# First phase of a hybrid decoder layer from a transposed x, the norm's factor applied to results, and other PSUM banks around the merge

## The chip, the cores and the metric

The kernel runs on one core of a Trainium2 chip. The metric is the device time of one execution in microseconds (us), lower is better. The core's engines are TensorE (PE in the profile; its weight loads are PEld), VectorE (DVE), ScalarE (ACT), GpSimd (POOL) and SyncE (SP), which here only issues DMA transfers.

## The reference

One layer on 512 tokens of width 1024, all in float32. A shared RMS-normalised input h goes through one wide projection, whose columns feed two branches: an mLSTM (queries and keys through a convolution, values v_ml, output gates o_ml, input and forget gates if_pre) and a sliding-window attention with 16 query and 4 key/value heads. The branches are merged with sigmoid gates, projected, and followed by an MLP and a gated embedding.

```python
def reference(x, p, norm_mix_g, w_in, conv_qk, b_if, mlstm_norm_g, sinks, w_branch_a, w_branch_b,
              w_out, norm_mlp_g, w_up, w_down, norm_ple_g, w_ple_gate, w_ple_proj, final_norm_g):
    h = rmsnorm(x, norm_mix_g[i])
    proj = h @ w_in[i]
    qk_ml, v_ml, o_ml, if_pre, q_sw, k_sw, v_sw, g_a, g_b = jnp.split(proj, split_idx, axis=-1)
    ...
    gates = (if_pre + b_if[i].astype(if_pre.dtype)).astype(jnp.float32)
    ...
    h_ml = mlstm_chunkwise(q_ml, k_ml, v_ml.reshape(B, S, ML_HEADS, ML_DV), ig, lf)
    ...
    y_a = jax.nn.sigmoid(o_ml) * h_ml
    y_b = swa_with_sinks(...)
    merged = jax.nn.sigmoid(g_a) * (y_a @ w_branch_a[i]) + jax.nn.sigmoid(g_b) * (y_b @ w_branch_b[i])
    x = x + merged @ w_out[i]
    u = rmsnorm(x, norm_mlp_g[i]) @ w_up[i]
    x = x + jnp.square(jax.nn.relu(u)) @ w_down[i]
    gate = jax.nn.sigmoid(rmsnorm(x, norm_ple_g[i]) @ w_ple_gate[i])
    x = x + gate * (p[i].astype(x.dtype) @ w_ple_proj[i])
    return rmsnorm(x, final_norm_g)
```

The norm multiplies each token's row by a factor r (one over the root of its mean square) and each column by norm_mix_g. Since r is one number for a token, h @ W equals r times ((x * norm_mix_g) @ W).

## The kernel before

**Products.** Every float32 operand is split into a high part (a cast to a shorter format, on ScalarE, L138) and a low part (the rest, a subtraction on VectorE, L139), by split (L135). Each product is three matmuls: high by high, high by low, low by high (pairs, L159; chain, L167, is the line of nearly every matmul). Weights come in pieces of 128x1024, 512 KB: load_w (L151) issues one DMA from SyncE into a buffer wr (four of them), casts into wh and subtracts into wl (four each). A piece is used by 24 matmuls of 512 columns.

**Start.** x arrives by token: four tiles xt of 128 tokens by 1024, with three pieces of w_vsif (the columns of the attention's values and of the eight gate inputs, 264 wide) queued between the first and the second. stir (L244) runs idle matmuls from the first instant. For each token tile, norm (L270) squares and sums on ScalarE and gives r; scaled (L281) multiplies by r and norm_mix_g on VectorE; turn (L286) transposes 128x128 blocks on TensorE; high (L294) and low (L298) split the result into hT, the normalised input with the 1024 columns on the partitions. products (L318) then makes the 128x264 block of values and gate inputs of that token tile, 24 matmuls into one PSUM bank, and values (L322) copies it out (vs, gt). A block manual_schedule (L330) fixes the order of TensorE, ScalarE and VectorE up to here; SyncE follows the text.

**Keys and output gates.** Two key products (L384) follow, split at once. Gate inputs are transposed (L420), and VectorE and ScalarE run scans over time on them (L424 to L447); their results are transposed again as gg and em (L502). o_proj (L411) makes eight output-gate products o0 to o7: 24 matmuls, a sigmoid on ScalarE into a tile sgo, a DMA from GpSimd to a DRAM tile god. o_bank (L404) gives o0, o1, o6, o7 a bank of the pool g and o2 to o5 the four banks of two two-bank tiles psa: o2 and o3 share one, o4 and o5 the other.

**vml.** The mLSTM values use a scheme of seven products instead of eight for a 2x2 block product (seven, L519). Its inputs are parts of hT (A11, A12, A22) and four sums S1 to S4 of such parts (h_sum, L470; their float32 source hf, L462, adds high and low part again; the split sums are hS).

**Merge.** For eight blocks, 24 matmuls of w_a, then VectorE multiplies by a gate (L920), GpSimd adds the other branch's term (L921), and the sum is split into mg. Then the PSUM pools close and a new pool pq opens with three two-bank pairs (pair, L936) and two single banks g. The w_out products (L951) go to two pairs for the first half of the columns, and to one pair and two g banks for the second (L958).

Outside the manual blocks a scheduler orders each engine's instructions by the text and by issue_after; each engine then runs its instructions strictly in that order, each waiting for what it needs.

Of the kernel before, what the change touches and what calls it, by code (L numbers as in the profile page):

```python
# [36 lines left out]
def block_kernel(  # L37
    ctx: ExitStack,
    tc: tile.TileContext,
    x: bass.AP,  # L40
    p: bass.AP,
# [183 lines left out]
    xt = [tk("xt")[:, :D] for _ in range(NT)]  # L225

    def load_x(m, n=1):
        for c in range(n):
            o = slice(c * D // n, (c + 1) * D // n)
            nc.sync.dma_start(out=xt[m][:, o], in_=x[m * P : (m + 1) * P, o])  # L230
# [13 lines left out]
    def stir(n):  # L244
        for i in range(n):
            tc.keep_in_program_order(T.matmul(idle[:, :P], ones, ones, start=True, stop=True))

    stir(9)
    gmix = [ps_a()[:, :512] for _ in range(2)]
    for c in range(2):  # L250
        T.matmul(gmix[c], ones, grow[:, c * 512 : (c + 1) * 512], start=True, stop=True)
    stir(2)
# [10 lines left out]
    vs = []  # L263
    gt = c1.tile([P, NT, 8], F32, name="gt")
    h2, hT = big_hl("h")
    hf = []
    xns = [tok_scratch("xn") for _ in range(NT)]
    rss = {}

    def norm(m):  # L270
        ss = small("ss", 1)
        A.activation(xns[m], xt[m], AF.Square, accum_out=ss)
        sd = small("sd", 1)
        A.activation(sd, ss, AF.Sqrt, bias=eps_t, scale=1.0 / D)
        rss[m] = small("rs", 1, 5)
        V.reciprocal(rss[m], sd)

    def scaled(m):
        for c in range(2):
            o = slice(c * 512, (c + 1) * 512)  # L280
            V.scalar_tensor_tensor(xns[m][:, o], xt[m][:, o], rss[m], gmix[c], ALU.mult, ALU.mult)  # L281

    def turn(m, kq):
        ps = ps_t()
        for k in range(4):
            T.transpose(ps[:, k * P : (k + 1) * P], xns[m][:, kq * 512 + k * P : kq * 512 + (k + 1) * P], ident)  # L286
        return ps

    def parts(m, kq):
        o = slice(4 * kq, 4 * kq + 4)  # L290
        return [t[:, o, m * P : (m + 1) * P] for t in h2]

    def high(m, kq, ps):
        return A.copy(parts(m, kq)[0], ps.rearrange("p (k c) -> p k c", k=4)).ins  # L294

    def low(m, kq, ps):
        hi, lo = parts(m, kq)
        return V.tensor_sub(lo, ps.rearrange("p (k c) -> p k c", k=4), r32(hi)).ins  # L298

    wvh = [wp.tile([P, 1024], F32R, tag="wh", bufs=WB, name=nm("wh"))[:, : n * 264] for _, n in vsif]  # L300
    wvl = [wp.tile([P, 1024], F32R, tag="wl", bufs=WB, name=nm("wl"))[:, : n * 264] for _, n in vsif]

    def w_high(i):
        A.copy(wvh[i], wv[i][:, : vsif[i][1] * 264])

    def w_low(i):
        V.tensor_sub(wvl[i], wv[i][:, : vsif[i][1] * 264], r32(wvh[i]))

    def products(m, order):
        ps = ps_g()  # L310
        where = {k0 + k: (i, k) for i, (k0, n) in enumerate(vsif) for k in range(n)}
        done = 0
        for kind, ks in order:
            for k in ks:
                i, c = where[k]
                act = hT[k][1 if kind == "lo h" else 0][:, m * P : (m + 1) * P]
                w = (wvl if kind == "lo w" else wvh)[i][:, c * 264 : (c + 1) * 264]
                last_mm[0] = T.matmul(ps[:, :264], act, w, start=done == 0, stop=done == 3 * KT - 1)  # L318
                done += 1
        return ps  # L320

    def values(m, ps):  # L322
        t = sp.tile([P, 256], F32, tag="vs", bufs=4, name=nm("vs"))
        A.copy(t, ps[:, :256])
        vs.append(t)
        return V.tensor_add(gt[:, m, :], ps[:, 256:264], bif)

    early, late, every = range(4), range(4, 8), range(8)
    plain = [("hi", early), ("lo w", early), ("lo h", early), ("hi", late), ("lo w", late), ("lo h", late)]
    with tc.manual_schedule(engines={mybir.EngineType.PE, mybir.EngineType.Activation, mybir.EngineType.DVE}):  # L330
        norm(0)
        w_high(0)
        scaled(0)
        w_low(0)
        t_ = [turn(0, kq) for kq in range(2)]
        high(0, 0, t_[0])
        low(0, 0, t_[0])
        w_high(1)
        high(0, 1, t_[1])
        w_low(1)  # L340
        low(0, 1, t_[1])
        w_high(2)
        w_low(2)
        norm(1)
        scaled(1)
        ps0 = products(0, [("hi", early), ("lo w", range(3)), ("lo h", early), ("hi", late), ("lo w", range(3, 8)), ("lo h", late)])
        t_ = [turn(1, kq) for kq in range(2)]
        norm(2)
        high(1, 0, t_[0])
        high(1, 1, t_[1])  # L350
        low(1, 0, t_[0])
        low(1, 1, t_[1])
        scaled(2)
        ps1 = products(1, plain)
        norm(3)
        values(0, ps0)
        scaled(3)
        t_ = [turn(2, kq) for kq in range(2)]
        q = [ps_a()[:, :512] for _ in range(2)]
        for kq in range(2):  # L360
            high(2, kq, t_[kq])
            low(2, kq, t_[kq])
        for kq in range(2):
            for k in range(4):
                T.transpose(q[kq][:, k * P : (k + 1) * P], xns[3][:, kq * 512 + k * P : kq * 512 + (k + 1) * P], ident)
        for kq in range(2):
            turned = [high(3, kq, q[kq]), low(3, kq, q[kq])]
        values(1, ps1)
        ps2 = products(2, plain)
        ps3 = products(3, plain)  # L370
# [8 lines left out]

    HALF = [slice(0, 64), slice(64, 128)]
    with tc.issue_after(turned[0]), tc.issue_after(turned[1]), tc.issue_after(turned[2]):
        keys = []  # L384
# [929 lines left out]
```

## Time and profile before

| | us |
|---|---|
| median of 3 runs (894.09 to 894.49) | 894.4 |
| the profiled execution | 894.35 |
| its span on the core | 892.5 |
| TensorE busy | 881.7 |
| VectorE busy | 646.3 |
| ScalarE busy | 450.2 |
| GpSimd busy | 24.3 |

The granted TensorE clock of the profiled run was 0.999 of full on average. The span is the time between the first and the last instruction that the profiler saw; the execution lasts 1.85 us longer. Busy times of different engines overlap. DMA moved 100.5 MB, 113 GB/s over the span, and was denser at the start: 284, 192 and 171 GB/s in the first three fortieths.

### The profile page before, as it was taken

The numbers are of one execution on the slowest core, as the hardware profiler recorded it, in microseconds if no ns is written. First come the engines' busy times: TensorE is split into PE (matmuls) and PEld (weight loads), VectorE is DVE, ScalarE is ACT, GpSimd is POOL, SyncE is SP. The second block draws the span as 40 slices with busy tenths as digits, with TensorE's granted clock in tenths as the row PEclk, the third lists the DMA queues.
The fourth block names the chain that finished last, engine by engine and source line by source line (L and its number), as shares of the span: only waits on it lengthen the run. The fifth ranks groups of instructions, "written<-read, shape, count | busy, mean of one in ns | idle before, by whom it ended". The sixth has DMA issues, their size and how long they took to land.

```text
span 892.5 us, 12113 instructions
## 1 busy us (share of the span) xinstructions
PE 881.7 (99%) x4672; PEld 740.2 (83%) x4672; DVE 646.3 (72%) x1029; ACT 450.2 (50%) x757; POOL 24.3 (3%) x42
## 2 busy tenths in 40 slices
PE   9999999999999999999999999999999999999996
PEld 8888899998878777788878888888888888888886
DVE  6875687864887887668634679757966885798466
ACT  6463444443667577764323545434434533444843
POOL 1011000000000000001300000000000000000000
PEclk9999999999999999999999999999999999999999
DMA  8552234335121232325353611630352054102402
GB/s 284 192 171 89 69 115 148 142 127 171 59 69 50 71 106 84 118 95 188 118 189 95 230 54 37 201 117 24 97 186 95 1 178 153 47 25 79 135 1 95
DMA packets 29965, 100.50 MB, mean 113 GB/s; under 512 B 4173, under 2 KB 4685, under 8 KB 29906
## 3 DMA queue, kind: packets, MB, share of 16 engines
q1 hardware_dynamic: 27938, 93.15, 31.3%
q0 software_dynamic: 1824, 6.30, 2.0%
q8 instruction: 37, 0.61, 0.3%
q10 hardware_dynamic: 144, 0.26, 0.1%
q14 instruction: 22, 0.18, 0.1%
HBM read 91.30 MB, written 8.40 MB: 112 GB/s over the span
## 4 chain that ended last, share of the span: by engine, by line
PE 77%; DVE 1%; ACT 0%; issue 0%; DVEq 0%
PE psg L167 37%; PE psp L167 23%; PE psg L768 8%; PE pst L167 2%; PE pst L743 1%; PE psa L696 1%; PE psa L730 1%; PE psa L167 1%; PE pst L842 1%; PE psp L947 1%; PE pst L894 0%; DVE gb L882 0%; DVE vh L139 0%; PE psp L989 0%; ACT wh L138 0%
## 5 line engine op out<-in xcount | busy, mean ns | idle before, releaser
L138 ACT CAST wh<-wr 128x1024 fp32r<-128x1024 f32 x134 | 140.6, 1052 | 209.0 <-PE psg L167 61.6
L139 DVE TENSOR_TENSOR wl<-wr,wh 128x1024 fp32r<-128x1024 f32 x134 | 168.5, 1262 | 100.8 <-ACT wh L138 93.8
L167 PE MATMUL psg<-x,wh 128*128 128x512 f32 x512 | 158.4, 390 | 0.0
L167 PE MATMUL psp<-wh,uf 128*128 128x512 f32 x448 | 139.1, 390 | 0.0
L167 PEld LDWEIGHTS psg<-x,wh 128*128 128x128 f32 x512 | 96.1, 188 | 19.8
L167 PE MATMUL psg<-x,wl 128*128 128x512 f32 x256 | 99.7, 389 | 0.0
L167 PEld LDWEIGHTS psp<-wh,uf 128*128 128x128 f32 x448 | 84.1, 188 | 17.4
L167 PE MATMUL psp<-wl,uf 128*128 128x512 f32 x224 | 87.2, 389 | 0.0
L138 ACT CAST wh<-wd 128x1024 fp32r<-128x1024 f32 x44 | 46.3, 1054 | 58.0 <-PE psp L167 26.3
L768 PE MATMUL psg<-h,wh 128*128 128x512 f32 x192 | 62.3, 399 | 0.0
L139 DVE TENSOR_TENSOR wl<-wd,wh 128x1024 fp32r<-128x1024 f32 x44 | 53.5, 1219 | 4.7 <-ACT wh L138 4.5
L167 PEld LDWEIGHTS psg<-x,wl 128*128 128x128 f32 x256 | 48.1, 188 | 9.9
L167 PE MATMUL psa<-h,wh 128*128 128x256 f32 (+1 forms) x256 | 55.2, 312 | 0.5 <-ACT p L617 0.4
L167 PEld LDWEIGHTS psp<-wl,uf 128*128 128x128 f32 x224 | 42.1, 188 | 8.6
L139 DVE TENSOR_TENSOR uf<-F,uf 128x1792 fp32r<-128x1792 f32 (+2 forms) x20 | 33.0, 1650 | 21.8 <-ACT uf L138 21.8
L167 PEld LDWEIGHTS psa<-h,wh 128*128 128x128 f32 x256 | 41.9, 191 | 4.0 <-ACT p L617 1.2
L167 PE MATMUL psg<-yb,wh 128*128 128x512 f32 x128 | 43.1, 408 | 0.3 <-DVE gb L882 0.2
L768 PEld LDWEIGHTS psg<-h,wh 128*128 128x128 f32 x192 | 35.4, 188 | 8.1 <-issue 0.4
L138 ACT CAST uf<-F 128x1792 fp32r<-128x1792 f32 (+2 forms) x20 | 27.9, 1397 | 26.4 <-DVE F L1023 26.2
L1009 DVE SCALAR_TENSOR_TENSOR rt<-psg,rB 128x512 f32<-128x512 f32 x32 | 22.0, 688 | 25.6 <-PE psg L167 25.6
L167 PE MATMUL psg<-ya,wh 128*128 128x512 f32 x128 | 40.5, 395 | 0.0
L167 PE MATMUL psg<-h,wh 128*128 128x512 f32 x128 | 39.9, 393 | 0.0
(289 smaller groups left out, 1729.7 us busy)
## 6 DMA issues: line engine op xcount, KB each, us to landing
wr<-in_w_up SPq DMA_DIRECT2D x32, 512.0 KB, 3.4
wd<-in_w_down SPq DMA_DIRECT2D x24, 512.0 KB, 4.3
wr<-in_w_o SPq DMA_DIRECT2D x8, 512.0 KB, 4.2
gd<-gr POOLq DMA_DIRECT2D x8, 512.0 KB, 2.9
wr<-in_w_qsw SPq DMA_DIRECT2D x8, 512.0 KB, 4.3
wr<-in_w_qkml SPq DMA_DIRECT2D x8, 512.0 KB, 3.4
wr<-in_w_b SPq DMA_DIRECT2D x8, 512.0 KB, 3.4
gl<-gd SPq DMA_DIRECT2D x8, 512.0 KB, 3.4
```

What stands on the lines that cost most here:

```text
L138: done = A.copy(dst[0], src)
L139: V.tensor_sub(dst[1], src, r32(dst[0]))
L167: last_mm[0] = T.matmul(ps, l, r, start=first and i == 0, stop=last and i == len(ops) - 1, skip_group_check=parts)
L696: T.matmul(o, q[x][HALF[ab], n * P : (n + 1) * P], keys[kp][y][HALF[ab], k0 : k0 + 256], start=i == 0, stop=i == 2)
L730: T.transpose(pt[:, c : c + P], lm3[:, g, j * P : (j + 1) * P], ident)
L743: T.matmul(o[HALF[ab], m * 256 : (m + 1) * 256], vs[n + m + 1 - nk + j][:, c : c + 64], pTs[m][:, j * 512 + ab * 256 : j * 512 + (ab + 1) ...
L768: T.matmul(ps, l, r, start=k == 0 and j == 0, stop=k == KT - 1 and j == 2)
L842: T.matmul(psc[:, n0:], qk[4 + h][:, n0 : n0 + P], qk[h][:, n0:], start=True, stop=True)
L947: T.transpose(ps[:, m * P : (m + 1) * P], xk[m][:, k * P : (k + 1) * P], ident)
L1009: V.scalar_tensor_tensor(a, ps, 0.0, rB, ALU.max, ALU.mult)
```

## The change

x is now passed twice, by token and transposed (x_t, four pieces of 256 columns by 512 tokens). Values, gate inputs, keys and the first three output gates are computed from xg, the split of x_t * norm_mix_g, which has no r in it. Tokens arrive later and only give the sums of squares. From these r4 (128x4, r of each token) is made; four matmuls of ones by a diagonal of r4 (psr) give rows, the factors of all 512 tokens on every partition. Values and gate inputs are multiplied by r4, keys (kt) and the first three output gates by rows. h_rows makes the normalised x in place and splits it into hT, which o3 to o7 and all that follows use. The values are made k by k into four banks. The manual block now runs to o4, and includes SyncE. S1 to S4 come from the normalised x itself. In the merge the add is on VectorE, and the new pool's two g banks are taken before the pairs.

```diff
+    gmix = cp.tile([P, KT], F32, name="gmix")
+    nc.scalar.dma_start(out=gmix, in_=g_mix)
...
-    load_x(0, 2)
-    nc.sync.dma_start(out=grow[:1, :], in_=g_mix)
-    vsif = [(0, 3), (3, 3), (6, 2)]
-    wv = [load_raw(w_vsif[0, :, k0 * 264 : (k0 + n) * 264], n * 264) for k0, n in vsif]
-    load_x(1)
-    load_x(2)
-    load_x(3)
+    xT = [tk("xT")[:, :D].rearrange("p (two c) -> p two c", two=2) for _ in range(4)]
+    vsif = [(0, 2), (2, 3), (5, 3)]
...
+    def o_close(i, ps, by=None):
+        t = act_f("sgo")
+        if by is not None:
+            last_v[0] = V.tensor_mul(t, ps, by).ins
+            ps = t
+
+        def gate():
+            A.activation(t, ps, AF.Sigmoid)
+            nc.gpsimd.dma_start(out=god[i // 2][:, i % 2, :], in_=t)
+
+        return gate
...
+    def x_split(k):
+        split(xg[k], x_part(k), gmix[:, k : k + 1])
...
+    def squares(m, t):
+        A.activation(t, t, AF.Square, accum_out=ss4[:, m : m + 1])
...
+    with tc.manual_schedule(engines={ENG.PE, ENG.Activation, ENG.DVE, ENG.SP}):
+        for i in range(10):
+            T.matmul(idle[:, :P], ones, ones, start=True, stop=True)
+        nc.sync.dma_start(out=xT[0][:, 0, :], in_=x_t[0, :, :S])
+        for i, (k0, n) in enumerate(vsif):
+            wv.append(load_raw(w_vsif[0, :, k0 * 264 : (k0 + n) * 264], n * 264))
+            if i == 0:
+                nc.sync.dma_start(out=xT[0][:, 1, :], in_=x_t[0, :, S:])
+            else:
+                nc.sync.dma_start(out=xT[i].rearrange("p a b -> p (a b)"), in_=x_t[i])
+        nc.sync.dma_start(out=xT[3].rearrange("p a b -> p (a b)"), in_=x_t[3])
+        kraw = [load_raw(w_ksw[0], KT * P)]
+        xm = [tok_scratch("xm") for _ in range(NT)]
+        for m in range(NT):
+            if m == 2:
+                kraw.append(load_raw(w_ksw[1], KT * P))
+            nc.sync.dma_start(out=xm[m], in_=x[m * P : (m + 1) * P, :])
...
+        sd4, r4 = small("sd", NT), small("r4", NT)
+        A.activation(sd4, ss4, AF.Sqrt, bias=eps_t, scale=1.0 / D)
+        V.reciprocal(r4, sd4)
+
+        vps = [t[:, :264] for t in four_a()]
+        for k in range(KT):
+            i, c = where[k]
+            w = [t[i][:, c * 264 : (c + 1) * 264] for t in (wvh, wvl)]
+            for j, (l, rt) in enumerate(pairs(xg[k], w)):
+                for m in range(NT):
+                    T.matmul(vps[m], l[:, m * P : (m + 1) * P], rt, start=k == 0 and j == 0, stop=k == KT - 1 and j == 2)
+        kps = [ps_t(), ps_t()]
+        for _ in products_of(kps[0], kw[0], xg):
+            pass
+        late = products_of(kps[1], kw[1], xg)
+        for _ in range(12):
+            next(late)
+        dg = act_f("dg")
+        psr = ps_g()
+        for m in range(NT):
+            o = slice(m * P, (m + 1) * P)
+            V.tensor_scalar_mul(dg[:, o], ident, r4[:, m : m + 1])
+            T.matmul(psr[:, o], ones, dg[:, o], start=True, stop=True)
+        for _ in late:
+            pass
+        ow = [load_w(w_o[0], KT * P, KT)]
+        rows = act_f("rows")
+        A.copy(rows, psr)
+        for m in range(NT):
+            t = sp.tile([P, 256], F32, tag="vs", bufs=4, name=nm("vs"))
+            A.activation(t, vps[m][:, :256], AF.Copy, scale=r4[:, m : m + 1])
+            vs.append(t)
+            V.scalar_tensor_tensor(gt[:, m, :], vps[m][:, 256:264], r4[:, m : m + 1], bif, ALU.mult, ALU.add)
+        h2, hT = big_hl("h")
+
+        def h_rows(i):
+            for j in range(2):
+                V.scalar_tensor_tensor(xT[i][:, j, :], xT[i][:, j, :], gmix[:, 2 * i + j : 2 * i + j + 1], rows, ALU.mult, ALU.mult)
+            split([t[:, 2 * i : 2 * i + 2, :] for t in h2], xT[i])
+
+        h_rows(0)
+        ow.append(load_w(w_o[1], KT * P, KT))
+        h_rows(1)
+        h_rows(2)
+        ow.append(load_w(w_o[2], KT * P, KT))
+        h_rows(3)
+        ow.append(load_w(w_o[3], KT * P, KT))
         for i in range(2):
-            ps = proj_T(w_ksw, i, ps_t)
+            t = act_f("kt")
+            V.tensor_mul(t, kps[i], rows)
             keys.append(act_hl("kk"))
-            split(keys[i], ps)
+            split(keys[i], t)
+        ops = [o_open(i, xg, ow[i]) for i in range(3)]
+        gates = [o_close(i, ops[i], rows) for i in range(3)]
+        rows_last = last_v[0]
+        ow.append(load_w(w_o[4], KT * P, KT))
+        for i in (3, 4):
+            gates.append(o_close(i, o_open(i, hT, ow[i])))
+            if i == 3:
+                o_last = last_mm[0].ins
+    for gate in gates:
+        gate()
...
+    with tc.issue_after(o_last):
+        pgi, pgf = ps_t(), ps_t()
...
-        G.tensor_tensor(sg, sg, t2[i], ALU.add)
+        V.tensor_add(sg, sg, t2[i])
...
+    first_g = [ps_g(), ps_g()]
...
-            pv = [a[:, 0, :], a[:, 1, :], ps_g(), ps_g()]
+            pv = [a[:, 0, :], a[:, 1, :], *first_g]
```

TensorE's first instructions, in the kernel before: idle matmuls (ones), transposes of a token tile (xn by ident), and the first products (h by the vsif weights wh and wl, into one bank).

```order
L246 MATMUL psg_122<-ones 128x128 x2
L286 MATMUL pst_163<-ident,xn_141 128x128 x4
L286 MATMUL pst_168<-ident,xn_141 128x128 x4
L318 MATMUL psg_189<-wh_145,h_139 128x264 x3
L318 MATMUL psg_189<-wh_146,h_139 128x264
L318 MATMUL psg_189<-wl_148,h_139 128x264 x3
```

The same place after; xg_116 and xg_117 are high and low part of the first 128 columns of x, psa_213 and psa_214 the four banks of the four token tiles.

```order
L306 MATMUL psg_108<-ones 128x128 x10
L348 MATMUL psa_213<-wh_171,xg_116 128x264 x2
L348 MATMUL psa_214<-wh_171,xg_116 128x264 x2
L348 MATMUL psa_213<-wl_172,xg_116 128x264 x2
L348 MATMUL psa_214<-wl_172,xg_116 128x264 x2
L348 MATMUL psa_213<-wh_171,xg_117 128x264 x2
L348 MATMUL psa_214<-wh_171,xg_117 128x264 x2
```

The transposes are gone, and the products go through all four token tiles before the next 128 columns.

VectorE behind the values, in the kernel before: the float32 sums hf, the subtractions of the two keys kk, the sums s, and the low parts wl of output-gate weights.

```order
L466 TENSOR_TENSOR hf_563<-h_139,h_140 128x1024
L139 TENSOR_TENSOR kk_392<-pst_360,kk_391 128x512
L474 TENSOR_TENSOR s_95_565<-hf_557 128x4x128
...
L139 TENSOR_TENSOR wl_614<-wr_611,wh_613 128x1024
L139 TENSOR_TENSOR wl_647<-wr_644,wh_646 128x1024
L139 TENSOR_TENSOR kk_427<-pst_395,kk_426 128x512
L424 COPY ig_456<-pst_446 4x512
```

The same place after; wl_414 and wl_424 are the low weights of o2 and o3, xT_106 the last block of h_rows, sgo_515 to sgo_519 the multiplied products of o0 to o2.

```order
L140 TENSOR_TENSOR wl_414<-wr_411,wh_413 128x1024
L375 SCALAR_TENSOR_TENSOR xT_106<-xT_106,gmix,rows_377 128x512 x2
L140 TENSOR_TENSOR h_392<-xT_106,h_391 128x1024
L140 TENSOR_TENSOR wl_424<-wr_421,wh_423 128x1024
L387 TENSOR_TENSOR kt_427<-pst_311,rows_377 128x512
L140 TENSOR_TENSOR kk_430<-kt_427,kk_429 128x512
L387 TENSOR_TENSOR kt_433<-pst_312,rows_377 128x512
L140 TENSOR_TENSOR kk_436<-kt_433,kk_435 128x512
L262 TENSOR_TENSOR sgo_515<-psg_439,rows_377 128x512
L262 TENSOR_TENSOR sgo_517<-psg_464,rows_377 128x512
L262 TENSOR_TENSOR sgo_519<-psa_489,rows_377 128x512
L140 TENSOR_TENSOR wl_524<-wr_521,wh_523 128x1024
```

Normalising x, both keys and three multiplications now stand in one row, with the weights of o1 to o3 between them and those of o4 behind.

ScalarE as vml begins, in the kernel before: sigmoids of o4 to o7 (sgo), casts of vml weights (wh), and the two copies p of the first product A11.

```order
L414 ACTIVATE sgo_707<-psa_610 128x512
L138 CAST wh_900<-wr_848 128x1024
L414 ACTIVATE sgo_761<-psa_610 128x512
L414 ACTIVATE sgo_795<-psg_764 128x512
L138 CAST wh_916<-wr_850 128x1024
L414 ACTIVATE sgo_829<-psg_798 128x512
L138 CAST wh_935<-wr_840 128x1024
L572 COPY p_164_892<-psa_856 128x512
L572 COPY p_165_894<-psa_856 128x512
```

The same place after; hS are the high parts of the sums, sgo_744, sgo_778 and sgo_812 the sigmoids of o5, o6 and o7.

```order
L139 CAST wh_918<-wr_823 128x1024
L139 CAST hS_677<-s_115_672 128x512
L139 CAST hS_681<-s_115_672 128x512
L139 CAST wh_936<-wr_825 128x1024
L139 CAST hS_685<-s_114_667 128x512
L139 CAST hS_689<-s_114_667 128x512
L266 ACT_TABLE_LOAD
L266 ACTIVATE sgo_744<-psa_490 128x512
L266 ACTIVATE sgo_778<-psg_753 128x512
L266 ACTIVATE sgo_812<-psg_787 128x512
L560 COPY p_159_875<-psa_839 128x512
L560 COPY p_160_877<-psa_839 128x512
```

The sigmoids of o5 to o7 stood among the weight casts and stand now behind four of the hS casts, one weight cast more (wh_936) and a table load.

## Rows read from the trace of the kernel before

**Rows 1.** The page's first part: busy time, share, instructions of each engine.

```profile
PE 881.7 (99%) x4672; PEld 740.2 (83%) x4672; DVE 646.3 (72%) x1029; ACT 450.2 (50%) x757; POOL 24.3 (3%) x42
```

**Rows 2.** Waits of TensorE, whole kernel: what waited for what: total, times, longest.

```profile
PE psp L167 <- ACT wh L138: 0.9, 1, 0.9
```

**Rows 3.** Timeline of TensorE, start: start, duration, instruction, count, idle before.

```profile
0.99 4.21 PE L246 MATMUL psg<-ones 128*128 128x128 f32 x18 [0.99 <-POOL ones L199]
...
8.82 1.14 PE L318 MATMUL psg<-wh,h 128*128 128x264 f32 x4
...
19.03 0.73 PE L318 MATMUL psg<-wh,h 128*128 128x264 f32 x4
...
24.92 0.62 PE L167 MATMUL pst<-h,wh 128*128 128x512 f32 x2
```

**Rows 4.** Timeline of TensorE in vml: A11, the first S2 matmuls, A12.

```profile
81.61 0.39 PE L167 MATMUL psa<-wh,h 128*128 128x512 f32 x1
...
87.05 0.39 PE L167 MATMUL psg<-wh,hS 128*128 128x512 f32 x1
...
88.41 0.47 PE L167 MATMUL psa<-wh,h 128*128 128x512 f32 x1
```

**Rows 5.** Timeline of TensorE, merge: the last w_a matmul, the first of w_out.

```profile
447.60 0.39 PE L167 MATMUL psg<-ya,wl 128*128 128x512 f32 x1
448.86 0.47 PE L167 MATMUL psp<-wh,mg 128*128 128x512 f32 x1 [0.88 <-ACT wh L138]
```

**Rows 6.** Timeline of SyncE's issues, start: three vsif pieces, then x.

```profile
2.08 1.29 SPq L148 DMA_DIRECT2D wr<-in_w_vsif  x3
3.41 1.71 SPq L230 DMA_DIRECT2D xt<-in_x  x3
```

**Rows 7.** DMA issues of 3.2 to 3.8 us: size, us from issue to landing.

```profile
xt<-in_x SPq DMA_DIRECT2D x1, 512.0 KB, 6.9
wr<-in_w_vsif SPq DMA_DIRECT2D x1, 264.0 KB, 6.0
```

**Rows 8.** Stretch table: length, busy PE, PEld, DVE, ACT, POOL, clock, DMA, GB/s.

```profile
8.80:24.80 16.00, 15.42 (x119) 14.33 (x120) 12.92 (x25) 11.88 (x23) 0.00 (x0) 1.00 0.81 286
```

**Rows 9.** Timeline of TensorE: ones by diagonal in a later norm, and what follows.

```profile
501.03 0.61 PE L989 MATMUL psp<-dg,ones 128*128 128x128 f32 x4
501.40 0.47 PE L167 MATMUL psg<-x,wl 128*128 128x512 f32 x1
```

**Rows 10.** Groups by shape, 0 to 130 us, ScalarE: busy, mean ns, idle before.

```profile
L138 ACT CAST wh<-wr 128x1024 fp32r<-128x1024 f32 x27 | 28.4, 1055 | 45.1 <-PE psa L167 15.5 <-PE psg L167 10.9 <-PE pst L167 7.1
...
L414 ACT ACTIVATE sgo<-psg 128x512 f32<-128x512 f32 x4 | 2.3, 593 | 0.0
...
L324 ACT COPY vs<-psg 128x256 f32<-128x256 f32 x4 | 1.5, 376 | 1.0 <-PE psg L318 1.0
...
L414 ACT ACT_TABLE_LOAD x1 | 1.3, 1283 | 0.0
```

**Rows 11.** The same view, VectorE.

```profile
L139 DVE TENSOR_TENSOR wl<-wr,wh 128x1024 fp32r<-128x1024 f32 x26 | 31.5, 1222 | 22.9 <-ACT wh L138 16.1 <-issue 6.5
...
L326 DVE TENSOR_TENSOR gt<-psg,bif 128x8 f32<-128x8 f32 x4 | 0.6, 157 | 0.1
```

**Rows 12.** Line 680, VectorE, operands in SBUF: shortest, median, longest ns.

```profile
L680 DVE SCALAR_TENSOR_TENSOR acc<-acc,sg x8: 682/684/685, 332.0 to 337.5; 128x512 f32<-128x512 f32 x8
```

**Rows 13.** Timeline of ScalarE: three hS casts in a row.

```profile
54.34 1.67 ACT L138 CAST hS<-s 128x512 fp32r<-128x512 f32 x3
```

**Rows 14.** Timeline of VectorE, merge: the last multiplication by the gate.

```profile
448.02 0.69 DVE L920 TENSOR_TENSOR sga<-psg,gl 128x512 f32<-128x512 f32 x1 [1.64 <-PE psg L167]
```

**Rows 15.** Timeline of TensorE: the last matmul of the kernel.

```profile
885.04 0.28 PE L167 MATMUL psg<-wh,x 128*128 128x256 f32 x1
```

**Rows 16.** Stretch table behind it (columns as rows 8; the clock stands third-last).

```profile
889.00:889.50 0.50, 0.00 (x0) 0.00 (x0) 0.00 (x0) 0.00 (x0) 0.00 (x0) 1.00 0.29 106
889.50:890.00 0.50, 0.00 (x0) 0.00 (x0) 0.00 (x0) 0.00 (x0) 0.00 (x0) 0.82 1.00 381
```

More of the change, by code (lines that the diff above doesn't have):

```diff
@@ L40, in block_kernel @@
     x: bass.AP,
+    x_t: bass.AP,
     p: bass.AP,
@@ L222, in cols @@
         return t
[L225 to L230, printed above, removed]
-    load_x(0, 2)
-    nc.sync.dma_start(out=grow[:1, :], in_=g_mix)
-    vsif = [(0, 3), (3, 3), (6, 2)]
-    wv = [load_raw(w_vsif[0, :, k0 * 264 : (k0 + n) * 264], n * 264) for k0, n in vsif]
-    load_x(1)
-    load_x(2)
-    load_x(3)
+    xT = [tk("xT")[:, :D].rearrange("p (two c) -> p two c", two=2) for _ in range(4)]
+    vsif = [(0, 2), (2, 3), (5, 3)]
+    where = {k0 + k: (i, k) for i, (k0, n) in enumerate(vsif) for k in range(n)}
     bif = c1.tile([P, 8], F32, name="bif")
-    nc.sync.dma_start(out=bif, in_=b_if.broadcast_to([P, 8]))
     idle = ps_g()
[L244 to L252, printed above, removed]
     def rstd_of(ss, n):
@@ L261, in rstd_of @@
         return rs
[L263 to L372, printed above, removed]
@@ L409, in o_bank, with o_open @@
         return obanks[i - 2]
-    def o_proj(i):
-        ps = proj_T(w_o, i, lambda: o_bank(i))
-        t = act_f("sgo")
-        A.activation(t, ps, AF.Sigmoid)
-        nc.gpsimd.dma_start(out=god[i // 2][:, i % 2, :], in_=t)
-    pgi, pgf = ps_t(), ps_t()
-    for m in range(NT):
-        T.transpose(pgi[:4, m * P : (m + 1) * P], gt[:, m, :4], ident)
-        T.transpose(pgf[:4, m * P : (m + 1) * P], gt[:, m, 4:], ident)
+    last_v = [None]
+    def o_open(i, acts, w):
+        ps = o_bank(i)
+        mm_T(ps, w, acts)
+        return ps
@@ new lines, in block_kernel, with x_part, w_split @@
+    xg = [act_hl("xg") for _ in range(KT)]
+    wv, wvh, wvl = [], [], []
+    ss4 = small("ss", NT)
+    def x_part(k):
+        return xT[k // 2][:, k % 2, :]
+    def x_split(k):
+        split(xg[k], x_part(k), gmix[:, k : k + 1])
+    def w_split(i):
+        n = vsif[i][1] * 264
+        wvh.append(wp.tile([P, 1024], F32R, tag="wh", bufs=WB, name=nm("wh"))[:, :n])
+        wvl.append(wp.tile([P, 1024], F32R, tag="wl", bufs=WB, name=nm("wl"))[:, :n])
+        split([wvh[i], wvl[i]], wv[i][:, :n])
@@ new lines, in block_kernel, with proj_T @@
+    for gate in gates:
+        gate()
+    gml = cols(g_ml, KT, "gml", c1)
+    gmlp = cols(g_mlp, KT, "gmlp")
+    gple = cols(g_ple, KT, "gple")
+    cw = cols(conv, KT * 4, "cw", c1)
+    sink = c1.tile([P, 16], F32, name="sink")
+    nc.sync.dma_start(out=sink, in_=sinks.broadcast_to([P, 16]))
+    def proj_T(wd, i, bank=ps_g):
+        ps = bank()
+        mm_T(ps, load_w(wd[i], KT * P, KT), hT)
+        return ps
+    with tc.issue_after(o_last):
+        pgi, pgf = ps_t(), ps_t()
+        for m in range(NT):
+            T.transpose(pgi[:4, m * P : (m + 1) * P], gt[:, m, :4], ident)
+            T.transpose(pgf[:4, m * P : (m + 1) * P], gt[:, m, 4:], ident)
```

96 lines of the change are left out of this document (50 added, 46 removed).

## The prediction

> **What bounds the kernel now.** I read the page first: TensorE is busy 881.7 of 892.5 us, VectorE 72%, ScalarE 50% [rows 1]. Then TensorE's waits: the longest late one is 0.9 us [rows 2]. So the end time is TensorE's own line of matmuls; a change counts only where it makes that line start earlier, grow, or stop. Then I read, stage by stage, what TensorE does where the change cuts in: the start [rows 3], vml [rows 4], the merge [rows 5]. The profiled execution took 894.35 us, 1.85 more than its span; I sum against 894.35, which is the median of 894.4 to within 0.05.
>
> **1. Keys start earlier.** Before, TensorE does its first product at 8.82 and, token block by token block, reaches the first key matmul at 24.92 [rows 3]. After, k by k, no normalised tile is needed. k=0 and 1 need the first 776 KB and are done early; k=2 needs the tile xT1, with which 256+264+256+396+512 = 1684 KB have been sent. In the queue before, 1572 KB had landed with the third vsif load (issued near 2.95 as the last of three from 2.08, 6.0 us to land: 8.95) and 2084 KB with the x tile behind it (3.41+6.9 = 10.3) [rows 6, 7]. Between them by bytes: 9.25. One 512-column cast, 0.59 to 0.62, gives 9.9. Then 72 matmuls (six k, four token blocks, three terms) at 0.123, which is (24.92-19.03)/48 [rows 3]: keys from 18.75, **-6.2**. The other tiles keep pace at the 286 GB/s of that stretch [rows 8] (xT2 near 12.5, used from 12.85). A landing 1.3 us off either way moves this term by as much.
>
> **2. The norm's factor.** Four matmuls of ones with a diagonal (psr) are added between 36 and 12 key matmuls. Four records of that kind took 501.40-501.03 = 0.37 [rows 9]; eight and the change of weights, **+0.9**. They need the tokens: 3.1 MB more after 12.9 at 286 GB/s is 23.9; square 1.05 (the pass of a 128x1024 cast [rows 10]) and small steps 0.8 give 25.8. TensorE gets there at 18.75+36x0.2267 = 26.9, at the pace of 24 matmuls in 87.05-81.61 [rows 4]. In time by 1.1 us. So psr ends at 27.8 and the keys at 30.5.
>
> **3. What is behind psr on VectorE.** Now h, keys and gates come late and in one row. psr read at 28.0, rows copied by 28.6 (0.59); four vs copies (0.376) and gt steps (0.157) in turn, about 1.8 [rows 10, 11]: 30.4. A block of h_rows is two SBUF steps (0.684 each, near enough 1.3 a pair [rows 12]), a cast 1.05, a subtraction 1.22 [rows 10, 11] and hand-overs: 3.6. Four blocks and three weight subtractions (1.15 when queued back to back) end at 48.25. Two keys, each multiply 0.69 [rows 14], cast 0.58, subtract 0.68: 52.3. Three sgo multiplies: 54.2.
> TensorE has 48 matmuls for o0 and o1 (10.9): at o2 by 41.4. o2's weights come between blocks 2 and 3: cast 42.2, subtraction 43.5. Idle 0.8 and 0.9, **+1.7**. o2 ends at 48.55. o3 writes the other half of o2's tile, psa_489's neighbour, and its first matmul waits for sgo_519, the last row of the VectorE piece shown with the diff: 54.25. **+5.7**. Both ends: nothing if that chain were 7.4 shorter, 8.6 in all if each block took 0.3 more. I take 7.4, since every pass in it has its own row. Behind the waiting matmul stand o3 to o7, everything. The transposes of gates, gg and em, now stand inside o7, and the gate transposes that feed them behind o4: TensorE has 56 matmuls between, 12.7 us, and the chain of scans has some eight small passes of about 0.67, two table loads of 1.28 [rows 10], two scans and up to three weight subtractions of 1.22 [rows 11], an estimate of 12.7 to 13.9. A wait of 0 to 1.2, I take **+0.8**.
>
> **4. vml.** In ScalarE's row the cast wh_936 now stands ahead of two hS casts, the table load and the sigmoids of o5, o6, o7. That cast needs the buffer of wh_859, free when A11's 24 matmuls end; the first S2 matmul needs the bank of o6, so it waits for sgo_778. From the end of A11: 0.2 drain, cast 1.05, hS twice 1.1, table load 1.28, two sigmoids 1.1 [rows 10, 13]: 4.7 of idle TensorE. After three matmuls A12 waits for the third sigmoid and two p copies, less what those matmuls cover: 0.85. **+5.55**. Before, TensorE steps from A11 to S2 and back to A12 with no gap (87.05, 88.41) [rows 4]. Lower end 4.7, if A12 does not wait again; upper end 6.2, if A12 waits for all three passes of 0.55 to 0.59 less nothing.
>
> **5. Merge.** Before, the first w_out matmul began at 448.86, 1.03 behind its turn (447.60+0.23) [rows 5]. The profile names the weight cast; but the VectorE multiply of the last w_a bank ran 448.02 to 448.71, and the first pair lay on that bank [rows 14]. With first_g opened ahead of the pairs, only x1's second half uses it: **-1.0**. The eight adds move from GpSimd to VectorE, 0.69 each; VectorE stood idle 1.64 before the last such multiply [rows 14], which hides them. Without that cover they would cost up to 5.5 on an engine busy 72% overall.
>
> Squares on ScalarE, bank names and the DMA for god change nothing on TensorE: they fall in gaps of engines that it does not wait for. The sum: -6.2+0.9+7.4+0.8+5.55-1.0 = **+7.4, or 901.8**, while the clock holds.
>
> **6. The clock.** [...]
>
> [...]
>
> **The rivals.**
> A, my forecast: only the stop before o3 costs clock, 901.8+1.3 = 903.1. For it: the idle time at the end [rows 16]. Chance 0.42.
> B: the clock holds through both, 901.8. For it: no stop over 1 us ever stood in this kernel's middle, so nothing shows a fall there. 0.25.
> C: both fall, 901.8+1.3+1.4 = 904.5. For it: the vml stop is close to the idle time of the end [rows 16], and three matmuls then a second short stop follow it. 0.20.
> D: the tokens land late and psr waits about 2 us with everything behind it, near 905. For it: only 1.1 us of margin against a rate that varies; against it: the loads are large and queued early. 0.05.
> E, the other side: VectorE and ScalarE passes in a row run far below their means. The place is the chain from psr to sgo_519, 26.2 us long. If passes take 28% less, the stops before o2 and o3 are gone (-7.4) and the whole change comes out at about zero; at 40% less vml's stop is 3.3 instead of 5.55 and the kernel ends at -6.2+0.9+0.8+3.3-1.0 = -2.2, **892.2**. For it: three hS casts in a row took 1.67, 0.557 each, 6% less than the 0.593 of a sigmoid of that size alone [rows 10, 13]. Against: 6% is not 28%. 0.05, with 0.03 for a result within 0.2%, near 894.
>
> **How the numbers follow.** The likeliest is A: 903.1. A to D are all slower: 0.92 by over 0.2% (1.8 us, about what a measurement of this kernel can tell from no change). Faster 0.05, same 0.03. The range: the landing (1.3) and the chain (0.7) below B give 900.0, and the same above C, with D, give 906.4. Outside lie E, the same, and some tails.
>
> **What would show it.** The first key matmul at 18 to 20 us. TensorE idle before the first o3 matmul by 5 to 6.5 us, named to VectorE, and about 1.7 before o2. In vml idle of 4 to 5 before S2 and about 0.9 before A12, both named to ScalarE. Lower granted clock in the 2 to 4 us behind the first stop, in A not behind the second. The gap before the first w_out matmul at about 0. No other new wait over 0.5 us. The prediction is wrong if o3 does not wait, if ScalarE has the sigmoids done before A11 ends, or if psr comes after 28 us.

## The result

| | us | against the kernel before, same chips |
|---|---|---|
| kernel before, median of 4 (893.68 to 894.49) | 894.25 | |
| changed kernel, median of 4 (905.94 to 907.72) | 907.38 | ratio 1.0145, 95% interval 1.0133 to 1.0157 |
| profiled execution of the changed kernel | 905.94, span 904.0 | |

The change costs 13.1 us by the medians, 11.6 by the two profiled executions. The forecast was 903.1, the range ended at 906.4: the sign and the places are right, the size is not. The transposed x is an input of the changed kernel, so the time of making it is in neither figure.

The profile after, first the page's line of busy times (as [rows 1]):

```profile
PE 882.1 (98%) x4642; PEld 740.3 (82%) x4642; DVE 650.5 (72%) x1050; ACT 457.2 (51%) x760; POOL 11.9 (1%) x33
```

TensorE's waits (as [rows 2]: what waited for what, total, times, longest):

```profile
PE psg L168 <- ACT sgo L266: 4.6, 1, 4.6
PE psa L168 <- DVE sgo L262: 3.8, 1, 3.8
PE psa L168 <- ACT wh L139: 1.4, 1, 1.4
PE pst L489 <- DVE gg L440: 1.4, 1, 1.4
PE psg L306 <- POOL ones L202: 1.0, 1, 1.0
PE psa L168 <- DVE wl L140: 0.7, 1, 0.7
```

TensorE's busy time is the same within 0.4 us, and the span is 11.5 longer: TensorE stands 11.1 us more. The equal sums of busy time hide that 30 matmuls are gone and that others run more slowly, as the clock below shows. Of the waits, all but the one on ones (the idle 0.99 of [rows 3]) are the stops that were forecast: vml's, the one before o3, the first before o2, the one in o7, the second before o2. The wait on the w_out weights is gone.

TensorE's timeline at those places (as [rows 3 to 5] and [rows 15]; start, duration, instruction, count, idle before and releaser):

```profile
18.54 0.62 PE L300 MATMUL pst<-xg,wh 128*128 128x512 f32 x2
...
26.71 1.05 PE L360 MATMUL psg<-dg,ones 128*128 128x128 f32 x8
...
30.34 0.62 PE L168 MATMUL psg<-xg,wh 128*128 128x512 f32 x2
...
42.80 0.73 PE L168 MATMUL psa<-xg,wh 128*128 128x512 f32 x2 [1.42 <-ACT wh L139]
44.25 0.79 PE L168 MATMUL psa<-xg,wl 128*128 128x512 f32 x1 [0.71 <-DVE wl L140]
...
54.89 1.19 PE L168 MATMUL psa<-h,wh 128*128 128x512 f32 x2 [3.81 <-DVE sgo L262]
...
82.67 0.19 PE L489 MATMUL pst<-ident,gg 4*128 4x4 f32 x1 [1.36 <-DVE gg L440]
...
87.66 0.39 PE L168 MATMUL psa<-wh,h 128*128 128x512 f32 x1
...
97.89 0.80 PE L168 MATMUL psg<-wh,hS 128*128 128x512 f32 x1 [4.63 <-ACT sgo L266]
...
460.56 0.39 PE L168 MATMUL psg<-ya,wl 128*128 128x512 f32 x1
460.78 0.39 PE L168 MATMUL psp<-wh,mg 128*128 128x512 f32 x1
...
896.79 0.28 PE L168 MATMUL psg<-wh,x 128*128 128x256 f32 x1
```

Subtracting the same places before gives where the time goes, one row for each place:

| place | before | after | shift | forecast A |
|---|---|---|---|---|
| first key matmul | 24.92 | 18.54 | -6.4 | -6.2 |
| first A11 matmul | 81.61 | 87.66 | +6.05 | +4.2 |
| first S2 matmul | 87.05 | 97.89 | +10.8 | +8.9 |
| last w_a matmul | 447.60 | 460.56 | +13.0 | +9.8 |
| first w_out matmul | 448.86 | 460.78 | +11.9 | +8.7 |
| last matmul | 885.04 | 896.79 | +11.75 | +8.7 |

The shift has its value by the end of vml. The forecast is short by 1.9 up to A11 and by another 1.3 within vml.

The clock there (the table by stretches, as [rows 16]; the clock stands third-last):

```profile
44.00:44.50 0.50, 0.25 (x1) 0.25 (x2) 0.50 (x2) 0.00 (x0) 0.00 (x0) 0.63 0.00 0
47.50:48.00 0.50, 0.50 (x4) 0.41 (x3) 0.50 (x2) 0.04 (x1) 0.00 (x0) 0.96 0.04 16
54.00:54.50 0.50, 0.00 (x0) 0.00 (x0) 0.50 (x2) 0.48 (x2) 0.00 (x0) 0.87 0.00 0
54.50:55.00 0.50, 0.11 (x1) 0.14 (x1) 0.50 (x2) 0.50 (x1) 0.00 (x0) 0.50 0.00 0
57.50:58.00 0.50, 0.50 (x3) 0.37 (x2) 0.50 (x3) 0.50 (x1) 0.50 (x2) 0.72 0.90 246
95.00:95.50 0.50, 0.00 (x0) 0.00 (x0) 0.50 (x1) 0.48 (x2) 0.00 (x0) 0.83 0.00 0
102.00:102.50 0.50, 0.50 (x3) 0.37 (x2) 0.00 (x0) 0.00 (x0) 0.00 (x0) 0.84 1.05 426
```

The granted clock fell from 1.00 to 0.50 at all three stops: from 44.1 to 47.5, from 54.4 to 57.8, from 95.3 to 102.2 (the ends are worked out from the half microseconds in which it changed). In those stretches a matmul takes about 0.43 instead of 0.227.

### The profile page after: what moved, and what is told of

The parts are those of the page before. It is cut to its first block, busy times and chain, and to the rows that moved or that the text cites. A ratio compares the mean times of both kernels' runs of the same rounds, so it can differ in the third digit from the quotient of the medians.

```text
span 904.0 us, 12043 instructions
## 1 busy us (share of the span) xinstructions
PE 882.1 (98%) x4642; PEld 740.3 (82%) x4642; DVE 650.5 (72%) x1050; ACT 457.2 (51%) x760; POOL 11.9 (1%) x33
## 4 chain that ended last, share of the span: by engine, by line
PE 77%; DVE 1%; ACT 0%; issue 0%; DVEq 0%
PE psg L168 37%; PE psp L168 23%; PE psg L756 7%; PE pst L168 2%; PE pst L731 1%; PE psa L684 1%; PE psa L718 1%; PE psa L168 1%; PE pst L830 1%; PE psp L937 1%; PE pst L882 0%; DVE gb L870 0%; DVE vh L140 0%; PE psp L979 0%; PE psg L1086 0%
## 5 line engine op out<-in xcount | busy, mean ns | idle before, releaser
L139 ACT CAST wh<-wr 128x1024 fp32r<-128x1024 f32 (+1 forms) x137 | 142.8, 1045 | 205.2 <-PE psg L168 66.1
L140 DVE TENSOR_TENSOR wl<-wr,wh 128x1024 fp32r<-128x1024 f32 (+1 forms) x137 | 165.9, 1214 | 99.0 <-ACT wh L139 98.7
L756 PE MATMUL psg<-h,wh 128*128 128x512 f32 x192 | 62.3, 399 | 0.0
L168 PE MATMUL psa<-h,wh 128*128 128x256 f32 (+1 forms) x240 | 51.3, 311 | 4.5 <-DVE sgo L262 3.8
L168 PEld LDWEIGHTS psa<-h,wh 128*128 128x128 f32 x240 | 39.5, 194 | 8.1 <-ACT wh L139 4.2
L703 ACT ACTIVATE lm<-lm,nmx 128x256 f32<-128x256 f32 (+1 forms) x64 | 30.0, 469 | 17.2 <-DVE nmx L696 15.6
```

The lines of the kernel that those rows point to most:

```text
L139: done = A.copy(dst[0], src)
L140: V.tensor_sub(dst[1], src, r32(dst[0]))
L168: last_mm[0] = T.matmul(ps, l, r, start=first and i == 0, stop=last and i == len(ops) - 1, skip_group_check=parts)
L703: A.activation(lm3[:, g, :], lm3[:, g, :], AF.Exp, bias=nmx[:, g : g + 1], accum_out=sm[:, g : g + 1])
L756: T.matmul(ps, l, r, start=k == 0 and j == 0, stop=k == KT - 1 and j == 2)
```

## The experiments

**The merge's part alone**, in the kernel before:

```diff
-        G.tensor_tensor(sg, sg, t2[i], ALU.add)
+        V.tensor_add(sg, sg, t2[i])
...
+    first_g = [ps_g(), ps_g()]
...
-            pv = [a[:, 0, :], a[:, 1, :], ps_g(), ps_g()]
+            pv = [a[:, 0, :], a[:, 1, :], *first_g]
```

> The kernel before with the merge's part of the change alone: the add on VectorE and the two g banks taken ahead of the pairs. Theory (the first w_out matmul waited for VectorE's last read of a w_a bank): the 1.03 us in front of it goes, nothing else moves, 894.3 - 1.0 = 893.3, and VectorE's eight adds of 0.69 stand in its idle time. Rival 1 (the wait was for the weight cast that the profile names): no change, 894.3. Rival 2 (the adds load VectorE): slower than 894.3, by up to 5.5.

Measured: 893.38 against 894.04, ratio 0.9990 (0.9981 to 0.9999). Its timeline of TensorE at the merge:

```profile
447.73 0.39 PE L167 MATMUL psg<-ya,wl 128*128 128x512 f32 x1
447.96 0.39 PE L167 MATMUL psp<-wh,mg 128*128 128x512 f32 x1
```

The first w_out matmul follows at 0.23, with no idle time. On ScalarE the weight cast of that moment, the one to which the profile had put the wait down, only begins:

```profile
447.98 1.06 ACT L138 CAST wh<-wr 128x1024 fp32r<-128x1024 f32 x1 [3.18 <-PE psg L167]
```

It ends 1.1 after the matmul that was said to wait for it has begun. So the wait was for the bank. The medians differ by 0.7, the interval goes from 0.1 to 1.7 and holds the gap's 1.0.

**The banks without the add** (the diff above without its first two lines):

> The kernel before with the two g banks taken ahead of the pairs, and the merge's add left on GpSimd. Theory (the banks make the gain of the merge's part): 893.4 as with the add on VectorE. Rival (it was the add): 894.1, as before.

Measured: 892.93 against 894.24, ratio 0.9986 (0.9977 to 0.9995). The banks make the gain. Moving the add to VectorE cannot be told from nothing: the subtraction beside it takes 2.34 here with the add on GpSimd, 1.22 with it on VectorE, and neither is waited for:

```profile
447.41 0.69 DVE L920 TENSOR_TENSOR sga<-psg,gl 128x512 f32<-128x512 f32 x1 [1.64 <-PE psg L167]
448.27 2.34 DVE L139 TENSOR_TENSOR wl<-wr,wh 128x1024 fp32r<-128x1024 f32 x1 [0.17 <-ACT wh L138]
```

**o3 in the other tile**, in the changed kernel:

```diff
-        return obanks[i - 2]
+        return obanks[{2: 0, 3: 2, 4: 3, 5: 1}[i]]
```

> The changed kernel with o3 in the other two-bank tile (o3 and o4 share one, o2 and o5 the other), so that its first matmul need not wait for the multiplication that reads o2. Theory (the stop before o3 is that wait, and the low clock behind it follows from the stop): the idle 3.8 us and 1.4 us of slow matmuls go, the next late thing is the normalised x at about 48 and o3's low weights at 49, while o2 ends near 50: 907.4 - 5.2 = 902.2, or to 901 if the gates' chain starts earlier too. Rival 1 (the slow matmuls are not due to the stop): only the idle goes, 903.6. Rival 2 (o3 is late for the normalised x anyway): 906 to 907.4.

Measured: 901.49, ratio 1.0080 (1.0065 to 1.0096), 5.9 less than the changed kernel (5.1 by the profiled executions). TensorE goes from o2 to o3 without a stop, at a granted clock of 1.00 (45 to 55). The wait in o7 is gone too, since the gates' chain starts earlier: its transposes stand at 55.73, behind o3, and in the changed kernel at 67.20, behind o4.

```profile
49.16 0.62 PE L168 MATMUL psa<-xg,wh 128*128 128x512 f32 x2
...
49.84 0.62 PE L168 MATMUL psa<-h,wh 128*128 128x512 f32 x2
...
93.33 0.80 PE L168 MATMUL psg<-wh,hS 128*128 128x512 f32 x1 [8.16 <-ACT sgo L266]
```

The normalised x was in time, so the wait before o3 was for the multiplication that reads the other half of the tile. But vml's stop grew from 4.6 to 8.2. TensorE came to A11 8.1 earlier (79.55 against 87.66), and ScalarE's sigmoids came only 4.6 earlier (92.19 against 96.75), since the casts ahead of them wait for VectorE's sums:

```profile
88.55 2.33 ACT L139 CAST hS<-s 128x512 fp32r<-128x512 f32 x4 [2.25 <-DVE s L463]
```

So some 3.5 of the 8.1 was lost again in vml, and that the time lies between the 901 and the 902.2 expected is partly luck. Some of what is gained at a stop is given back at the next.

**The sigmoids of o5 to o7 first**: in the changed kernel the splits of S3 and S4 are issued behind the sigmoid of o7.

```diff
...
-        S3 = h_split(s3)
-        S4 = h_split(s4)
...
     for i in range(5, 8):
         o_proj(i)
+    with tc.issue_after(last_s[0]):
+        S3 = h_split(s3)
+        S4 = h_split(s4)
```

> The changed kernel with the splits of S3 and S4 issued behind the sigmoid of o7, so that ScalarE has the sigmoids of o5 to o7 done before the cast that waits for the end of A11. Theory (the stop in vml is ScalarE's order): the idle 4.6 us before the first S2 matmul goes and with it 2.2 us of slow matmuls: 907.4 - 6.8 = 900.6. Rival 1 (another thing is as late there, the weights' low parts on VectorE): 904 to 907. Rival 2 (the slow matmuls stay): 902.8.

Measured: 903.70, ratio 1.0103 (1.0089 to 1.0117), 3.7 less by the medians, 2.1 by the profiled executions; the first figure, 6.8, was missed. The sigmoids are out of the way, and the next late thing is 1.9 behind: the low part of S2's weights on VectorE, which is what rival 1 named, with 904 to 907. Its timeline of TensorE:

```profile
43.97 0.50 PE L168 MATMUL psa<-xg,wl 128*128 128x512 f32 x1 [0.72 <-DVE wl L140]
...
54.61 1.19 PE L168 MATMUL psa<-h,wh 128*128 128x512 f32 x2 [5.32 <-DVE sgo L262]
...
96.67 0.50 PE L168 MATMUL psg<-wl,hS 128*128 128x512 f32 x1 [1.93 <-DVE wl L140]
```

A side result: here the clock held at 1.00 (40 to 50) through the stop before o2, which is 1.41 and 0.72 long, in the changed kernel 1.42 and 0.71. o2 ran faster, the wait before o3 is 5.3 instead of 3.8, and o3 begins at 54.6 as before. So the slow matmuls of o2 cost the changed kernel nothing: its wait before o3 was 1.5 shorter for them. But behind the stop before o3 the clock stayed low until 60.0 here, in the changed kernel until 57.8: o3 and o4 together took 13.5 (54.61 to 68.14) instead of 12.3 (54.89 to 67.20), and vml began 0.9 later, at 88.59. That is part of what the gain lacks.

**Idle matmuls in the stops**, in the changed kernel (12 before o2, 28 before o3, and 24 behind A11, which the lines below do not show):

```diff
...
+        def fill(bank, n):
+            for _ in range(n):
+                T.matmul(bank[:, :P], ones, ones, start=True, stop=True)
...
+        fill(obanks[2], 12)
+        ops.append(o_open(2, xg, ow[2]))
+        fill(obanks[2], 28)
...
```

> The changed kernel with idle matmuls of ones, 128 columns, put into the three stops: 12 before o2, 28 before o3, 24 before the first S2 product. They add no useful work; every wait stays. Theory (the stops let TensorE's clock fall, and that costs by itself): granted clock 1.0 through all three; 1.4 us behind the stop before o3 are gained, about 1.4 behind the one in vml (2.2 of slow matmuls less 0.8 of a wait of A12 that comes back), 907.4 - 2.8 = 904.6. Rival 1 (the slowness behind the stops has another cause): 907.4. Rival 2 (the added matmuls run longer than the stops): above 907.4.

Measured: 903.19 (902.80 to 903.55), ratio 1.0099 (1.0085 to 1.0113): 4.2 less than the changed kernel by the medians, 2.4 by the profiled executions. It does more and takes less time. Its timeline of TensorE, in which each idle matmul is two records:

```profile
49.80 6.41 PE L390 MATMUL psa<-ones 128*128 128x128 f32 x56
55.97 0.71 PE L168 MATMUL psa<-h,wh 128*128 128x512 f32 x2
...
92.84 5.52 PE L525 MATMUL pst<-ones 128*128 128x128 f32 x48
98.11 0.48 PE L168 MATMUL psg<-wh,hS 128*128 128x512 f32 x1
```

Its table by stretches:

```profile
54.00:58.00 4.00, 4.00 (x29) 3.67 (x29) 4.00 (x9) 3.97 (x6) 1.21 (x2) 1.00 0.16 32
95.00:102.00 7.00, 7.00 (x48) 6.36 (x47) 6.32 (x7) 4.01 (x7) 1.61 (x3) 1.00 0.74 235
```

The clock stays at 1.00 and the matmuls behind the stops run at 0.227 each: the slowness came from the stops. The idle matmuls ran longer than the stops, by some 0.7 before o3 (VectorE's multiplication of o2 ended at 55.16; in the changed kernel o3 began 0.15 behind that, here at 55.97) and by some 0.5 in vml; without that the profiled 903.55 would be near 902.4. The sum of the prediction without the clock is 901.8. That the two are so near is partly luck: the sum lacks 0.6 before o3 and 0.9 in o7 (below), and has 0.85 for a second wait in vml that is not in this trace.

**gg and em later**: in the changed kernel their transposes stand behind vml.

```diff
-    pgc = ps_t()
-    with tc.issue_after(last_mm[0].ins):
...
     vml()
...
+    pgc = ps_t()
+    with tc.issue_after(last_mm[0].ins):
```

> The changed kernel with the transposes of gg and em moved out of o7, behind vml (their results are needed later). Theory 1 (vml's stop hangs on the end of A11, by way of the cast that waits for A11's weight buffer): the 1.4 us wait inside o7 and the 0.3 behind it go, vml's stop stays at 4.6: 907.4 - 1.7 = 905.7. Theory 2 (vml's stop ends when VectorE has worked off what the normalised x and the sums left it): TensorE comes to vml 1.7 earlier and waits 1.7 longer there, 6.3 in place of 4.6: 907.4, or worse by what the order changes.

Measured: 909.03, ratio 1.0164 (1.0149 to 1.0180), 1.6 more by the medians. The profile fell on the slowest execution, 910.88, and is 4.9 above that of the changed kernel. The wait in o7 is gone and vml's stop went from 4.6 to 9.6:

```profile
101.92 0.80 PE L168 MATMUL psg<-wh,hS 128*128 128x512 f32 x1 [9.59 <-ACT sgo L266]
```

ScalarE's timeline tells why:

```profile
97.14 2.33 ACT L139 CAST hS<-s 128x512 fp32r<-128x512 f32 x4 [3.67 <-DVE s L463]
99.48 1.28 ACT L266 ACT_TABLE_LOAD   x1
...
101.27 1.08 ACT L266 ACTIVATE sgo<-psg 128x512 f32<-128x512 f32 x2
```

The four casts wait for VectorE's last sums, and the sigmoids stand behind them. Neither theory's time was met (905.7, 907.4): the stop ends when VectorE's sums do, as the second has it, and the new order put those sums later still.

**Both repairs together** (the other tile, and the sigmoids first):

> The changed kernel with both repairs: o3 in the other tile, and the splits of S3 and S4 behind the sigmoid of o7. If the two add up as measured apart (-5.9 and -3.7): 897.8. If vml's stop was 8.2 with the banks alone because the sigmoids stood behind sums that VectorE makes late: more than that, down to 894.5, since the whole 8.2 less what VectorE's weights cost (1.9) and the low clock (2.2) go. If VectorE's backlog sets vml's start whatever ScalarE's order: 901.5, as with the banks alone.

Measured: 899.09, ratio 1.0054 (1.0040 to 1.0068). Between the first figure and the last: together the two give 8.3 of the 9.6 that they gave apart. TensorE's timeline in vml:

```profile
86.81 0.50 PE L168 MATMUL psg<-wh,hS 128*128 128x512 f32 x1 [0.83 <-ACT sgo L266]
92.92 0.50 PE L168 MATMUL psg<-wl,hS 128*128 128x512 f32 x1 [2.63 <-DVE wl L140]
97.63 0.50 PE L168 MATMUL psa<-wh,h 128*128 128x512 f32 x1 [2.15 <-ACT p L561]
```

One stop of 8.2 has become three of 5.6 together: a sigmoid, the low parts of weights, then the copies of A11's result behind other casts.

**A combined version**: o0 to o3 from the unnormalised halves, so that the normalised x is needed one gate later and no matmul writes the tile that a multiplication reads; the weights of o2 one block earlier; sigmoids first; gg and em behind vml.

```diff
...
         ow.append(load_w(w_o[1], KT * P, KT))
         h_rows(1)
-        h_rows(2)
         ow.append(load_w(w_o[2], KT * P, KT))
-        h_rows(3)
+        h_rows(2)
         ow.append(load_w(w_o[3], KT * P, KT))
+        h_rows(3)
+        ow.append(load_w(w_o[4], KT * P, KT))
...
-        ops = [o_open(i, xg, ow[i]) for i in range(3)]
-        gates = [o_close(i, ops[i], rows) for i in range(3)]
+        ops = [o_open(i, xg, ow[i]) for i in range(4)]
+        gates = [o_close(i, ops[i], rows) for i in range(4)]
...
```

> A version of the changed kernel: o0 to o3 from the unnormalised halves (in the changed kernel o0 to o2), the weights of o2 ahead of the third block of normalising, the splits of S3 and S4 behind the sigmoid of o7, gg and em transposed behind vml. Theory (the early start of 6.4 less 0.8 for the norm's factor, and 1.0 at the merge, are real and only the stops spent them): no stop before o2, o3 or in o7, normalised x at about 49 against o4's turn at 52; 894.2 - 6.6 = 887.6 without a stop in vml, 891 with one of 2 and low clock behind it. Rival (the early start cannot be kept, since VectorE is behind by what it does later than before): 894 or more.

Measured: 893.44 against 894.24, ratio 0.9993 (0.9984 to 1.0002). No stop is left up to vml, and the first A11 matmul comes at 74.38, 7.2 before that of the kernel before (part of that comes from the transposes of gg and em, which now stand behind vml). But in vml S2's low weights are 4.0 late and the clock falls; at the last w_a matmul nothing is left of the lead (447.84 against 447.60). The time lies between the theory's 891 with a stop and the rival's 894. The timeline of TensorE:

```profile
79.82 0.71 PE L168 MATMUL psg<-wh,hS 128*128 128x512 f32 x2
84.50 0.79 PE L168 MATMUL psg<-wl,hS 128*128 128x512 f32 x1 [3.96 <-DVE wl L140]
```

The table by stretches:

```profile
85.00:86.00 1.00, 1.00 (x4) 0.72 (x3) 1.00 (x2) 0.00 (x0) 0.00 (x0) 0.50 0.00 0
```

**The same with the last sums written behind A12's matmuls**:

```diff
...
             prod(X, A12, form(b21[i]), i, False, True)
+            if not S3:
+                with tc.issue_after(a11):
+                    more_sums()
...
```

> The combined version with VectorE's sums for S3 and S4 issued behind A11, so that the low weights of A12 and S2 come first. In the combined version before it, TensorE waited 4.6 us there for VectorE and ran with a low clock behind it. Theory (VectorE's order, not its load, made that wait): what is left is a wait of A12 for the copies of A11's result, about 0.8, clock held: 893.4 - 4.6 + 0.8 - 1.2 = 888.4. Rival (VectorE's load: the same passes are late wherever they stand): 891 to 894.

Measured: 888.81 (888.34 to 889.79) against 893.77, ratio 0.9941 (0.9928 to 0.9955): faster than both kernels, and at the figure expected, but not by the way expected. VectorE's order stayed: S2's low weights still stand behind the sums, at 83.69. What moved is TensorE's and ScalarE's order: A12, whose weights are ready, now follows two matmuls of S2, and the copies of A11's result stand ahead of the other casts. TensorE's timeline:

```profile
80.27 0.71 PE L168 MATMUL psg<-wh,hS 128*128 128x512 f32 x2
81.60 0.50 PE L168 MATMUL psa<-wh,h 128*128 128x512 f32 x1 [0.62 <-ACT p L552]
...
87.17 0.39 PE L168 MATMUL psg<-wl,hS 128*128 128x512 f32 x1
```

VectorE's timeline:

```profile
82.34 1.42 DVE L461 TENSOR_TENSOR s<-xT 128x256 f32<-128x256 f32 x4
83.69 1.22 DVE L140 TENSOR_TENSOR wl<-wr,wh 128x1024 fp32r<-128x1024 f32 x1
```

A12 fills the time in which S2's weights are late. So neither VectorE's order nor its load was tried apart here. What is shown is that with the new order of the products on TensorE and of the copies on ScalarE some 4 us of vml are gone (from the first A11 to the last w_a matmul 369.2 instead of 373.5); which of the two orders made it was not tried apart.

**The changed kernel again**, for a second profile, without an edit:

> The changed kernel again, for a second profile. Its first profile fell on its fastest execution, 905.94, the other three took 907.2 to 907.7. If the difference lies in where the clock falls and rises around the stops (theory), this profile shows the same waits within 0.3 us but other stretches of low clock, before o3 or in vml, that make up what differs. Rival (transfers at the start): first key matmul more than 1 us later than 18.54.

Measured: 906.92 (906.20 to 908.57), ratio 1.0149 (1.0135 to 1.0162). The profile again fell on the fastest execution, 906.20, with the same waits (4.6, 3.8, 1.4, 1.4) and the first key matmul at 18.73, 0.2 later. Why the others take 1 to 2 us more stays open; that the kernel with filled stops varies by 0.75 only, against 1.8 and 2.4 here, fits the clock as the cause and does not show it. Two figures speak against it, without settling it: the mean granted clock is 0.991 in all eight executions of the changed kernel, and the kernel before, which has no such stops, varied by 1.8 too in 15 executions (893.53 to 895.34).

## Why the prediction missed

**Keys earlier: right.** 18.54 against 18.75; k=2 began at 9.72 against 9.9. **The norm's factor: right.** psr at 26.71 against 26.9 with its diagonal in time, o0 at 30.34 against 30.5, so 0.8 against 0.9.

**The chain behind psr: right in kind, 0.6 short.** o3 began at 54.89 against 54.25. Of this the copies and gt steps are 0.4: VectorE came to the first block at 30.84, not 30.4. The stops before o2 were 2.1, not 1.7. The stop before o3 reads 3.8, not 5.7, only because o2's own matmuls ran slowly until 47.5; where they didn't, it was 5.3. The run with o3 in the other tile shows the wait's cause.

**The transposes in o7: too small.** I took 0.8. Measured was 1.4 of wait and some 0.3 of pieces behind it, in addition to the slow matmuls: the gate transposes start the chain behind o4, so a later TensorE makes the chain as much later. That is 0.9 too little. With o3 in the other tile, where they stood behind o3, the chain was done in time.

**vml: right in kind.** The idle time is 4.63 against 4.7, named to the sigmoid, by the way that ScalarE's order gave. The second part, 0.85 for A12, did not appear as a wait but under slow matmuls.

**The merge: right.** The gap of 1.03 is gone, the shift falls from 12.96 to 11.92, and the run with the merge's part alone shows the bank, not the weight cast, as the cause.

**The clock: the step that failed most.** I took the idle time at the end of the kernel before as what a stop must reach before it costs clock, called the 4.7 in vml close to it, and gave 0.42 to one fall and 0.20 to two; the 1.7 before o2 I did not weigh at all. By [rows 15 and 16] the clock had held for 4.5 us behind the last matmul (885.32 to 889.82, from the 0.82), so by them too 4.7 was longer. In the changed kernel it fell at all three stops, and sooner: after 0.6 us of idle time in the second piece of the stop before o2, after 3.3 before o3, after 2.1 in vml, at 95.3, while TensorE still waited. The 27 matmuls of S2 and A12 took from 97.89 to 106.22, 8.33 instead of 27 x 0.227 = 6.1. So vml cost 7.0 (4.8 and 2.2) instead of 5.55. No run shows the 1.3 and the 1.4 that A and C add for the clock; measured were 1.4 behind the stop before o3 and 2.2 in vml. The run with filled stops shows the clock as the cause of these. So the places of the stops were right, and what failed is the term for what they cost in clock.

With the right case, C, the forecast would have been 904.5; with the 0.6 of the chain and the 0.9 of o7, 906.0, which is the profiled execution. C's two terms for the clock are 0.9 less than the measured 1.4 and 2.2, and its 0.85 for A12 is not in the trace: the two errors nearly cancel. The median lies 1.4 above 906.0, and where these 1.4 are spent stays open. The range ended 1.9 above C and left the median 1.0 outside; its ends as its own terms add up, 2.0 below B and above C, are 899.8 and 906.5, which leaves the median outside too. "In A not behind the second stop" was the sign that I had named for telling A from C, and the trace shows lower clock there: 0.50 behind each of the three stops. It did not fall at every such stop: with o3 in the other tile and with the sigmoids first, the clock stayed at 1.00 through the stop before o2.

**The rivals.** B is refuted: the granted clock fell. D too: psr came on time, its diagonal done at 23.2. E, passes in a row far below their means, is refuted by o3's start, later than summed.
